# Zero fillings behind the first scaling, and another lane order in a triangular solve: one core, hybrid decoder step

## The chip, the cores and the metric

The kernel runs on one core of a Trainium2 chip. The metric is the device time of one execution in microseconds (us); the time given for a kernel is the median of several executions. The engines are TensorE (PE, with its weight loads listed apart as PEld), VectorE (DVE), ScalarE (ACT), GpSimd (POOL) and SyncE (SP), which issues most transfers.

## The reference

One layer of a decoder over a prompt of 2048 tokens and 8 sequences of 4 new tokens, width 1024, all in fp32. A normalised input `h` is projected to twelve column blocks; a short gated convolution and an RWKV-7 recurrence (16 heads of 64 x 64 state) run beside each other, are gated, projected and added to the input, and a last normalisation follows. What matters here is the recurrence:

```python
def step(S, inp):
    r_t, k_t, v_t, d_t, kk_t, a_t = inp
    sa = jnp.einsum('bhvk,bhk->bhv', S, -kk_t)
    S = (S * d_t[:, :, None, :] + sa[..., None] * (kk_t * a_t)[:, :, None, :]
         + v_t[..., None] * k_t[:, :, None, :])
    y = jnp.einsum('bhvk,bhk->bhv', S, r_t)
    return S, y
```

and the normalisation with which every row begins: `x * rsqrt(mean(x * x) + 1e-6) * g`.

## The kernel before

**Tiling.** The prompt is worked in four sets of 512 tokens. For each set and each pair of heads (8 pairs, so 32 pairs in all) PE projects the columns that the pair needs. Each fp32 product is made of three passes (high part by high part, low by high, high by low), so the operands are split: `XH` and `XL` are the high and low parts of the normalised, transposed input, and `whl` holds both parts of a weight block. A projection is a run of 24 matmuls into a PSUM tile `ip`.

**The recurrence** goes in chunks of 64 tokens, 8 chunks per set. Per pair five stages run as side work between the projections of other columns: `rwkv_keys`, `rwkv_solve`, `rwkv_merge`, `rwkv_load` and `rwkv_chain`. The keys stage makes decayed keys (`AR`, `BK`). The solve stage multiplies them on PE, masks the result into `GM` (on DVE), and inverts the unit triangular matrix of each chunk. It does this in 32 x 32 blocks: a pair has 2 heads x 2 diagonal blocks x 8 chunks = 32 blocks. ACT collects them in `Mc` (the partition holds head, block and row; the free axis chunk and column). DVE transposes `Mc` into `Mi` (128 x 1024, each element copied four times, for four groups of columns), and solves with 31 row steps on DVE: `tt<-Mi,X` multiplies, `X<-X,tt` adds. `X` starts as a copy of the constant `X0`, the identity in the layout of the solve, and holds eight groups of four solved rows. A lane (a partition within a group of 32) stands for one chunk and one of four row offsets. At the end DVE transposes `X` back:

```python
Xo = rw.tile([P, 32, 32], F32, name="Mi")[:, 0:8]
V.transpose(Xo.rearrange("p c (a e) -> p a e c", e=4), X)
```

`Xo` lies in a buffer of the name Mi, so the profile shows this transpose as `Mi<-X`, and the one before the solve as `Mi<-Mc`. Before the change the lane is (row offset e, chunk c), with the chunk running fastest; the transpose back puts chunk c's rows together by writing each element to an address of its own.

`rwkv_merge` copies the four groups of blocks of `Xo` into the block diagonal of `Xbd` on ACT (`Xbd<-Mi`, four copies of 32 x 256), transposes the first ones on DVE (`Mc<-Xbd`), and joins the 32 x 32 inverses to 64 x 64 ones with 32 small matmuls on PE (`pt<-Mc,GM`, then `pt<-Xbd,X`). `rwkv_chain` then carries the state `S` over the chunks: PE makes `pa`, DVE `UB`, PE `pb`, ACT `SV`, PE `pb`, DVE `S`.

**The start.** Four row tiles of 128 tokens are loaded into borrowed buffers (`GM` two, `BKt`, `SV`). ACT sums their squares, DVE and POOL take the root (`nw`, `rstd`), DVE scales one tile and ACT the other (`GM<-GM,rstd`), PE transposes them (`ip<-ident,GM`), and DVE, ACT and POOL split the result into XH and XL. `setup["scaled"][0]` is the DVE scaling of the first tile. `zero_rest` fills with zeros, on POOL, the parts of tiles that later steps read but never write (`UP`, `BK`, `AR`, `Xbd`, `UB`, `SV`, `S`): 18 fillings.

**What sets the order.** Each engine executes its own queue in order. The code records what it issues while a planner (`Clock`) interleaves main work and side work, and DVE and ACT instructions are then fixed in the planned order. `behind_of(b, a)` adds one more rule: instruction b is placed behind a. With `NoSync` this orders queues only; with `Sync` b also waits until a is done. All compute instructions are issued through one helper and so carry the line L264 in the profile; transfers carry L337.

Of the kernel before, what the change touches and what calls it, by code (L numbers as in the profile page):

```python
# [7 lines left out]
F32 = mybir.dt.float32  # L8
# [3 lines left out]
ALU = mybir.AluOpType  # L12
# [4 lines left out]
P = 128  # L17
# [4 lines left out]
NCH = 8  # L22
# [322 lines left out]
def hybrid_kernel(tc, x_prompt, x_sample, state_conv, state_shift, state_rwkv, norm_g, w_in, conv_w,  # L345
# [5 lines left out]
    V, A, G, T = (Traced(e, n, clock) for e, n in ((nc.vector, "DVE"), (nc.scalar, "ACT"), (nc.gpsimd, "POOL"), (nc.tensor, "PE")))  # L351
# [15 lines left out]
    TW = NT + 64  # L367
# [37 lines left out]

    order = []
    raws, parts_, lows = {}, {}, []
    setup = {"casts": [], "lows": [], "scaled": {}}
    state = {"use": 0, "dma": 0, "split": 0}

    def w_advance(dma, split, load):
# [198 lines left out]
    tmp = Ring(ph1.enter_context(tc.tile_pool(name="tmp", bufs=1)), [P, NT + 64], 8, clock)  # L610
# [62 lines left out]
    for hr in range(2):  # L673
        for q in range(2):
            sl = mask_p[hr * 64:(hr + 1) * 64, q]
            G.affine_select(out=sl, in_=sl, pattern=[[1, 64]], compare_op=ALU.is_gt if q == 0 else ALU.is_ge,
                            fill=0.0, base=0, channel_multiplier=-1)
# [3 lines left out]
    for hr in range(2):  # L681
        sl = seqm[hr * 64:(hr + 1) * 64, :]
# [9 lines left out]
                        in1=seqm.unsqueeze(2).broadcast_to([P, NS, SL]), op=ALU.mult)  # L692

    X0 = con.tile([P, 8, 32], F32, name="X0")
    xo0 = tmp.tile([P, TW], F32, name="tmp")[:, 0:256].rearrange("p (a b c) -> p a b c", b=4, c=8)
    G.memset(xo0, 1.0)
    for g in range(4):
        sl = xo0[g * 32:(g + 1) * 32]
        G.affine_select(out=sl, in_=sl, pattern=[[-4, 8], [-1, 4], [0, 8]], compare_op=ALU.is_equal, fill=0.0,
                        base=0, channel_multiplier=1)  # L700
    V.transpose(X0.rearrange("p a b -> p (a b)"), xo0.rearrange("p a b c -> p (a b c)"))
    tmp.free(xo0)

    rst = con.tile([P, NT], BF16, name="rst")
# [496 lines left out]
    col = [slice(32 * b, 32 * b + 32) for _ in range(2) for b in range(2)]  # L1201
    blk = [(slice(64 * h + 32 * b, 64 * h + 32 * b + 32)) for h in range(2) for b in range(2)]

    def rwkv_solve(th, p, o):

        AR = o["AR"]
        samp = th == LAST
        GM = GMB[(th * NB + p) % 2]


        yield 0.0, (), 2
        for c0 in range(0, NCH + samp, 4):
            cs = range(c0, min(NCH + samp, c0 + 4))
            pp = [new_pt([P, 512], F32, name="pt") for _ in range(2)]
            for c in cs:
                for h in range(2):
                    T.matmul(pp[h][:, (c - c0) * P:(c - c0 + 1) * P], lhsT=BK[HS[h], c].rearrange("p q t -> p (q t)"),
                             rhs=AR[HS[h], c].rearrange("p q t -> p (q t)"), start=True, stop=True)
            k = len(cs)
            mk = mask_s if c0 == NCH else mask_p  # L1220
            for h in range(2):
                V.tensor_tensor(out=GM[:, c0:c0 + k, :, h, :],
                                in0=pp[h][:, 0:k * P].rearrange("p (c a t) -> p c a t", a=2, t=64),
                                in1=mk.unsqueeze(1).broadcast_to([P, k, 2, 64]), op=ALU.mult)
            yield W["score"], (), 2 if c0 + 4 < NCH + samp else 0


        Mc = rw.tile([P, NCH, 32], F32, name="Mc")
        for i, g in enumerate(blk):
            h, b = i // 2, slice(i % 2 * 32, i % 2 * 32 + 32)  # L1230
            A.copy(Mc[g], GM[b, 0:NCH, 0, h, b])
        yield 0.5, [Mc]
        Mi = rw.tile([P, 32, 32], F32, name="Mi")
        V.transpose(Mi.rearrange("p t (e c) -> p t e c", c=NCH),
                    Mc.rearrange("p c t -> p t c").unsqueeze(2).broadcast_to([P, 32, 4, NCH]))
        X = rw.tile([P, 8, 32], F32, name="X")
        A.copy(X, X0)
        Mo = rw.tile([P, NCH, 32], F32, name="Mo")
        A.copy(Mo[64:96], GM[0:32, 0:NCH, 0, 1, 32:64])
        yield W["inv0"], [Mi, X]  # L1240

        for j in range(31, 0, -1):
            c0 = j // 4
            if c0 == 7:
                V.scalar_tensor_tensor(out=X[:, 7, 0:j], in0=Mi[:, j, 0:j], scalar=X[:, 7, j:j + 1], in1=X[:, 7, 0:j],
                                       op0=ALU.mult, op1=ALU.add)
                yield W["inv"]
                continue
            tt = sm.tile([P, 80], F32, name="tt")
            tv = tt[:, 0:(8 - c0) * j].rearrange("p (c i) -> p c i", i=j)  # L1250
            V.tensor_tensor(out=tv, in0=Mi[:, j, 0:j].unsqueeze(1).broadcast_to([P, 8 - c0, j]),
                            in1=X[:, c0:8, j:j + 1].broadcast_to([P, 8 - c0, j]), op=ALU.mult)
            V.tensor_tensor(out=X[:, c0:8, 0:j], in0=X[:, c0:8, 0:j], in1=tv, op=ALU.add)
            yield W["inv"]
        Xo = rw.tile([P, 32, 32], F32, name="Mi")[:, 0:8]
        V.transpose(Xo.rearrange("p c (a e) -> p a e c", e=4), X)
        o.update(GM=GM, Xo=Xo, Mo=Mo)
        yield W["inv"]

    def rwkv_merge(th, p, o):  # L1260

        GM, Xo, Mo = (o[k] for k in ("GM", "Xo", "Mo"))
        Xbd = o["Xbd"] = XB[(th * NB + p) % 2]
        samp = th == LAST
        for i, g in enumerate(blk):
            A.copy(Xbd[g, 0:NCH, col[i]], Xo[g])

        T11 = rw.tile([P, NCH, 32], F32, name="Mc")
        V.transpose(T11[0:96], Xbd[0:96, 0:NCH, col[0]])
        yield W["bt"], [T11[0:96], Mo[64:96]], 1  # L1270
        Wm = rw.tile([P, 8, 32], F32, name="X")
        pt = new_pt([P, 512], F32, name="pt")
        for c in range(NCH):
            for h in range(2):
                T.matmul(pt[blk[2 * h + 1], c * 32:(c + 1) * 32], lhsT=Mo[64:96, c, :] if h else GM[0:32, c, 0, 0, 32:64],
                         rhs=T11[blk[2 * h], c, :], start=True, stop=True)
        for h in range(2):
            A.copy(Wm[blk[2 * h + 1]], pt[blk[2 * h + 1], 0:NCH * 32].rearrange("p (c t) -> p c t", t=32))
        yield W["bt"], [Wm[32:128], Xbd[32:128]], 1
        pt = new_pt([P, 512], F32, name="pt")  # L1280
        for c in range(NCH):
            for h in range(2):
                T.matmul(pt[blk[2 * h], c * 32:(c + 1) * 32], lhsT=Wm[blk[2 * h + 1], c, :],
                         rhs=Xbd[blk[2 * h + 1], c, col[1]], start=True, stop=True)
        for h in range(2):
            A.copy(Xbd[blk[2 * h], 0:NCH, col[1]],
                   pt[blk[2 * h], 0:NCH * 32].rearrange("p (c t) -> p c t", t=32))
        yield W["bt"], (), samp
        if samp:
            for h in range(2):  # L1290
                V.tensor_copy(Xbd[HS[h], NCH, HS[h]], GM[0:64, NCH, 0, h, :])

            M = Xbd[:, NCH, :]
            pt = new_pt([P, 512], F32, name="pt")
            T.transpose(pt[:, 0:P], M, ident)
            MT = sm.tile([P, P], F32, name="sq")
            A.copy(MT, pt[:, 0:P])
            V.tensor_tensor(out=M, in0=M, in1=ident, op=ALU.add)
            yield W["samp"], [M, MT], 1
            for _ in range(SL - 2):  # L1300
                pt = new_pt([P, 512], F32, name="pt")
                T.matmul(pt[:, 0:P], lhsT=MT, rhs=M, start=True, stop=True)
                V.tensor_tensor(out=M, in0=pt[:, 0:P], in1=ident, op=ALU.add)
                yield W["samp"], [M], 1
        yield W["merge"], [Xbd]
# [440 lines left out]
    St = [xp.tile([P, P], F32, name=f"S{p}") for p in range(NB)]  # L1746
# [6 lines left out]
    scv = xp.tile([P, NB, 2 * NS], F32, name="scv")  # L1753
    def zero_rest():
        for t in (UP[64:128, 1].bitcast(F32), UP[0:64, 3].bitcast(F32), BK[:, NCH], ARB[0][:, NCH], ARB[1][:, NCH], *XB, *UB, SV[:, NCH]):
            G.memset(t, 0.0)
        for p in range(NB):
            G.memset(St[p], 0.0)
        yield 1

    def end_(th, p):
# [35 lines left out]
    for th, hv, p, nx in plan:  # L1797
# [15 lines left out]
        e = EDGE / 2 * NB  # L1813
# [15 lines left out]
    SP.flush(0)  # L1829
    clock.planning = False  # L1830

    def behind_of(b, a):
        tc.add_manual_dep(b, a.name, mybir.DependencyInfo(
            mybir.DependencyClass.NoSync, mybir.DependencyReason.DATA), reason="keep_in_program_order")

    for ops in clock.begun.values():
        ops.sort(key=lambda o: o[0])
        for (_, a), (_, b) in zip(ops, ops[1:]):
            behind_of(b, a)
    for b in setup["lows"]:  # L1840
        behind_of(b, setup["scaled"][0])
    behind_of(setup["casts"][1], setup["scaled"][1])

    ph1.close()
# [372 lines left out]
```

## Time and profile before

| | |
|---|---|
| median of 3 runs | 3048.32 us (3045.91 to 3054.13) |
| the profiled execution's own time | 3047.81 us |
| its span, first to last instruction | 3046.1 us |
| mean granted TensorE clock | 0.997 |
| POOL, DVE, ACT busy | 316.0, 2162.4, 1346.3 us |

A row of a group reads: engine, operation, output<-inputs by the program's names, shape, count, then busy us, mean ns of one, and the idle time of the engine before them with what ended it. A row of the timeline reads: start in us, length in us, engine, instruction, and in brackets the idle time before it. A row of stretches reads: from:to, length, then busy us and count for PE, PEld, DVE, ACT and POOL, the granted PE clock, the DMA share and GB/s.

### The profile page before, as it was taken

To read this page: it belongs to the slowest core of one execution; us is meant where nothing else is said; L and a number is where in the kernel's file an instruction comes from. 1 tells how busy PE (TensorE), PEld (TensorE's weight loads), DVE (VectorE), ACT (ScalarE), POOL (GpSimd) and SP (SyncE) were. 2 spreads that over 40 slices of the span, in tenths; PEclk is the share of its full clock that TensorE was granted. 3 is DMA by queue.
4 is the path that set the end of the run, shared out by engine and by line. 5 is a ranking of instruction groups with operands and counts; after the bars stand their busy time and mean duration, and the time that the engine had idled before them with its cause. 6 is when DMAs were issued, how large, how long until landed. Compare 5 with 4: busy or idle time off the path is not lost. (4 is left out here: it accounts for less than half of the span.)

```text
span 3046.1 us, 56137 instructions
## 1 busy us (share of the span) xinstructions
PE 2986.0 (98%) x21370; PEld 2559.5 (84%) x21370; DVE 2162.4 (71%) x5504; ACT 1346.3 (44%) x2745; POOL 316.0 (10%) x520
## 2 busy tenths in 40 slices
PE   8999999999999999999999999999999999999998
PEld 6778777788888788788787899999999997888996
DVE  6777778767777777777777777667767744486575
ACT  4555555554444445444444444444444322324223
POOL 2011111011111111111111110000100000000000
PEclk9999999999999999999999999999999999999999
DMA  8877767766666667666666665444343588898775
GB/s 273 289 236 237 251 220 248 230 223 228 208 218 210 209 218 240 223 222 216 216 221 212 198 215 179 149 136 146 127 145 130 170 267 317 325 324 295 271 264 195
DMA packets 319731, 678.05 MB, mean 223 GB/s; under 512 B 47610, under 2 KB 179827, under 8 KB 269798
## 3 DMA queue, kind: packets, MB, share of 16 engines
q1 hardware_dynamic: 310758, 670.27, 64.9%
q10 hardware_dynamic: 8704, 4.20, 0.5%
q8 instruction: 169, 2.77, 0.4%
q14 instruction: 100, 0.82, 0.1%
HBM read 479.10 MB, written 195.28 MB: 221 GB/s over the span
## 5 line engine op out<-in xcount | busy, mean ns | idle before, releaser
L264 PE MATMUL ip<-XH,whl 128*128 128x512 f32 (+3 forms) x6832 | 1853.9, 351 | 5.8 <-DVE whl L264 3.8
L264 PEld LDWEIGHTS ip<-XH,whl 128*128 128x128 f32 x6832 | 1174.5, 189 | 137.1 <-DVE whl L264 6.8
L264 PE MATMUL ip<-XL,whl 128*128 128x512 f32 (+3 forms) x3416 | 1195.4, 350 | 0.0
L264 PEld LDWEIGHTS ip<-XL,whl 128*128 128x128 f32 x3416 | 646.8, 189 | 65.0 <-issue 5.5
L264 DVE SCALAR_TENSOR_TENSOR S<-pb,pe,sp 64x64 f32<-64x64 f32 x512 | 143.1, 279 | 98.1 <-PE pb L264 91.5
L264 DVE TENSOR_TENSOR X<-X,tt 128x60 f32<-128x60 f32 (+21 forms) x864 | 187.7, 217 | 27.9
L264 DVE TENSOR_TENSOR tt<-Mi,X 128x60 f32<-128x60 f32 (+21 forms) x864 | 188.9, 219 | 24.9
L264 ACT ACTIVATE sp<-S,pe 128x128 f32<-128x128 f32 x256 | 102.4, 400 | 205.6 <-DVE S L264 204.5
L264 ACT COPY SV<-pb 64x128 f32<-64x128 f32 x256 | 66.1, 258 | 283.8 <-PE pb L264 279.7
L264 DVE TENSOR_TENSOR UB<-pa,P 64x64 f32<-64x64 f32 x512 | 110.2, 215 | 109.9 <-PE pa L264 92.3
L264 ACT ACTIVATE tmp<-ip,vec 128x512 f32<-128x512 f32 (+2 forms) x174 | 103.0, 593 | 181.0 <-PE ip L264 175.7
L264 PE MATMUL acc<-XH,whl 128*128 128x264 f32 (+1 forms) x800 | 141.2, 329 | 0.5 <-DVE tmp L264 0.5
L264 PEld LDWEIGHTS acc<-XH,whl 128*128 128x128 f32 x800 | 119.0, 188 | 14.9 <-DVE tmp L264 0.7
L264 PE MATMUL acc<-UA,whl 128*128 128x264 f32 (+1 forms) x720 | 117.7, 324 | 1.9 <-DVE My L264 1.9
L264 PEld LDWEIGHTS pb<-UB,Xbd 128*128 128x128 f32 x512 | 85.0, 188 | 40.1 <-PE ip L264 15.5
L264 PEld LDWEIGHTS acc<-UA,whl 128*128 128x128 f32 x720 | 105.0, 190 | 13.4 <-DVE My L264 2.3
L264 DVE TENSOR_TENSOR whl<-wraw,whl 128x1024 fp32r<-128x1024 f32 x81 | 101.7, 1255 | 19.6 <-ACT whl L264 18.9
L264 DVE TENSOR_TENSOR GM<-pt,mask_p 128x512 f32<-128x512 f32 x128 | 82.6, 686 | 42.9 <-PE pt L264 42.5
L264 PE MATMUL pb<-UB,Xbd 128*128 128x128 f32 x512 | 105.0, 286 | 8.1 <-DVE UB L264 7.0
L264 PEld LDWEIGHTS pa<-S,AR 128*128 128x128 f32 x512 | 86.7, 188 | 26.3 <-DVE S L264 14.7
L264 PE MATMUL acc<-XL,whl 128*128 128x264 f32 (+1 forms) x616 | 108.6, 326 | 0.0
L264 PEld LDWEIGHTS pb<-SV,BKt 128*128 128x128 f32 x512 | 89.4, 188 | 20.6 <-ACT SV L264 6.5
(559 smaller groups left out, 4422.9 us busy)
## 6 DMA issues: line engine op xcount, KB each, us to landing
wraw<-in_w_in_dram SPq DMA_DIRECT2D x81, 512.0 KB
whl<-w_k SPq DMA_DIRECT2D x24, 1024.0 KB
whl<-w_r SPq DMA_DIRECT2D x24, 1024.0 KB
whl<-w_v SPq DMA_DIRECT2D x24, 1024.0 KB
whl<-w_z SPq DMA_DIRECT2D x24, 1024.0 KB
whl<-w_xin SPq DMA_DIRECT2D x24, 1024.0 KB
whl<-w_cg SPq DMA_DIRECT2D x24, 1024.0 KB
whl<-w_zc SPq DMA_DIRECT2D x24, 1024.0 KB
```

What stands on the lines that cost most here:

```text
L264: r = f(*a, **k)
```

## The change

Two things. The zero fillings of `zero_rest` wait (with a semaphore) until the first row tile has been scaled on DVE. And the lane of the solve becomes (chunk c, row offset e), with e fastest, so a chunk's four solved rows stand in neighbouring lanes. The constant `X0` is made to fit. The transpose into `Mi` now reads each element of `Mc` four times in succession, the transpose back is plain, and the ACT copies into `Xbd` bring the rows into order by reading runs of four elements.

```diff
-    xo0 = tmp.tile([P, TW], F32, name="tmp")[:, 0:256].rearrange("p (a b c) -> p a b c", b=4, c=8)
+    xo0 = tmp.tile([P, TW], F32, name="tmp")[:, 0:256].rearrange("p (a c b) -> p a c b", b=4, c=8)
...
-        G.affine_select(out=sl, in_=sl, pattern=[[-4, 8], [-1, 4], [0, 8]], compare_op=ALU.is_equal, fill=0.0,
+        G.affine_select(out=sl, in_=sl, pattern=[[-4, 8], [0, 8], [-1, 4]], compare_op=ALU.is_equal, fill=0.0,
...
         Mi = rw.tile([P, 32, 32], F32, name="Mi")
-        V.transpose(Mi.rearrange("p t (e c) -> p t e c", c=NCH),
-                    Mc.rearrange("p c t -> p t c").unsqueeze(2).broadcast_to([P, 32, 4, NCH]))
+        V.transpose(Mi.rearrange("p t (c e) -> p t c e", c=NCH),
+                    Mc.rearrange("p c t -> p t c").unsqueeze(3).broadcast_to([P, 32, NCH, 4]))
...
         Xo = rw.tile([P, 32, 32], F32, name="Mi")[:, 0:8]
-        V.transpose(Xo.rearrange("p c (a e) -> p a e c", e=4), X)
+        V.transpose(Xo.rearrange("p a b -> p (a b)"), X.rearrange("p a b -> p (a b)"))
...
         for i, g in enumerate(blk):
-            A.copy(Xbd[g, 0:NCH, col[i]], Xo[g])
+            A.copy(Xbd[g, 0:NCH, col[i]].rearrange("p c (a e) -> p c a e", e=4),
+                   Xo[g].rearrange("p a (c e) -> p c a e", e=4))
...
     def zero_rest():
         for t in (UP[64:128, 1].bitcast(F32), ..., *XB, *UB, SV[:, NCH]):
-            G.memset(t, 0.0)
+            r = G.memset(t, 0.0)
+            setup["zeros"].append(r.ins)
         for p in range(NB):
-            G.memset(St[p], 0.0)
+            setup["zeros"].append(G.memset(St[p], 0.0).ins)
...
+    for b in setup["zeros"]:
+        behind_of(b, setup["scaled"][0], mybir.DependencyClass.Sync)
     for b in setup["lows"]:
         behind_of(b, setup["scaled"][0])
```

No instruction changes its place in any queue. On POOL, at the start, the first filling has one more semaphore to wait for, that of DVE; the other fillings and the XL subtractions stand behind it in the same queue. The piece of the difference (`UP` is the first filled tile, `rstd` the root, `carry` a one-column copy):

```order
@@ -26,5 +26,5 @@
 L264 TENSOR_TENSOR rstd<-nw_285,mhalf 128x2 [waits DVE_49,Pool_49]
 L264 COPY tmp<-carry 128x1
-L264 MEMSET UP 64x128 [waits Pool_49]
+L264 MEMSET UP 64x128 [waits DVE_49,Pool_49]
 L264 MEMSET UP 64x128
 L264 MEMSET BK 128x128 [waits Pool_49]
```

Nothing moved; the second filling and all behind it now start after the DVE scaling.

On DVE, at the end of the first pair's solve, the last row step (`tt`, `X`), the transpose back (`Mi<-X`) and the merge's transpose (`Mc<-Xbd`) stand as before; only the shape of the write differs:

```order
@@ -166,5 +166,5 @@
 L264 TENSOR_TENSOR tt<-Mi,X 128x8 [waits DVE_49]
 L264 TENSOR_TENSOR X<-X,tt 128x8 [waits DVE_49]
-L264 STREAM_TRANSPOSE Mi<-X 128x32x8 [waits DVE_49]
+L264 STREAM_TRANSPOSE Mi<-X 128x256 [waits DVE_49]
 L264 SCALAR_TENSOR_TENSOR tmp<-ip,omu,tmp 128x512 [waits Activation_49,Pool_49]
 L264 STREAM_TRANSPOSE Mc<-Xbd_218 96x256 [waits Activation_49]
```

Nothing moved here either, and it is the same in the other 31 pairs.

More of the change, by code (lines that the diff above doesn't have):

```diff
@@ L407, in hybrid_kernel @@
     raws, parts_, lows = {}, {}, []
-    setup = {"casts": [], "lows": [], "scaled": {}}
+    setup = {"casts": [], "lows": [], "scaled": {}, "zeros": []}
     state = {"use": 0, "dma": 0, "split": 0}
@@ L698, in hybrid_kernel @@
         sl = xo0[g * 32:(g + 1) * 32]
-        G.affine_select(out=sl, in_=sl, pattern=[[-4, 8], [-1, 4], [0, 8]], compare_op=ALU.is_equal, fill=0.0,
+        G.affine_select(out=sl, in_=sl, pattern=[[-4, 8], [0, 8], [-1, 4]], compare_op=ALU.is_equal, fill=0.0,
                         base=0, channel_multiplier=1)
-    V.transpose(X0.rearrange("p a b -> p (a b)"), xo0.rearrange("p a b c -> p (a b c)"))
+    V.transpose(X0.rearrange("p a b -> p (a b)"), xo0.rearrange("p a c b -> p (a c b)"))
     tmp.free(xo0)
@@ L1830, in hybrid_kernel, with behind_of @@
     clock.planning = False
-    def behind_of(b, a):
-        tc.add_manual_dep(b, a.name, mybir.DependencyInfo(
-            mybir.DependencyClass.NoSync, mybir.DependencyReason.DATA), reason="keep_in_program_order")
+    def behind_of(b, a, kind=mybir.DependencyClass.NoSync):
+        tc.add_manual_dep(b, a.name, mybir.DependencyInfo(kind, mybir.DependencyReason.DATA), reason="keep_in_program_order")
     for ops in clock.begun.values():
```

## The prediction

> **What bounds the kernel now.** I read the page first (busy shares, then the chain that ended last), then who waited for whom on TensorE, then two places in the timeline: the start, and the end of one pair's triangular solve.
>
> ```profile
> span 3046.1 us, 56137 instructions
> PE 2986.0 (98%) x21370; PEld 2559.5 (84%) x21370; DVE 2162.4 (71%) x5504; ACT 1346.3 (44%) x2745; POOL 316.0 (10%) x520
> ```
>
> TensorE (PE) is busy for 2986.0 of 3046.1 us, and the change takes no matmul away. So it can gain only from the 60.1 us in which PE stands idle, and from stretches in which PE's clock is low. Who ends the idle time of PE:
>
> ```profile
> PE ip L264 <- DVE GM L264: 11.2, 1, 11.2
> PE pt L264 <- DVE Mc L264: 7.3, 9, 2.1
> PE pb L264 <- DVE UB L264: 7.0, 17, 1.3
> PE ip L264 <- DVE whl L264: 3.8, 5, 1.3
> PE pa L264 <- DVE S L264: 3.3, 8, 0.8
> PE pt L264 <- DVE Yc L264: 2.5, 4, 1.2
> ```
>
> (us in total, times, longest.) The first row is the start: PE waits for the scaled rows in GM. The second is the merge: its first small matmuls wait for Mc, the transposed blocks that the solve leaves. These two rows lie straight behind the two edited places. The other four are waits for VectorE (DVE) in general.
>
> **The start.** DVE has to finish the root of the rows' mean square (nw, rstd) and scale the rows (GM) before PE can transpose them. DVE first, then GpSimd (POOL) with the zero fillings, then PE:
>
> ```profile
> 9.03 3.14 DVE L264 TENSOR_SCALAR nw<-nw 128x2 f32<-128x2 f32 x1
> 12.20 0.16 DVE L264 TENSOR_TENSOR rstd<-rstd,nw 128x2 f32<-128x2 f32 x1
> 12.40 1.33 DVE L264 TENSOR_SCALAR GM<-GM,rstd 128x1024 f32<-128x1024 f32 x1
> ...
> 22.55 0.17 DVE L264 TENSOR_SCALAR nw<-nw 128x2 f32<-128x2 f32 x1
> ...
> 22.96 0.75 DVE L264 TENSOR_SCALAR BKt<-BKt,rstd 128x1024 f32<-128x1024 f32 x1
> ```
>
> ```profile
> 8.81 0.45 POOL L264 MEMSET UP<- 64x128 f32 x2
> ...
> 12.08 1.79 POOL L264 MEMSET S<- 128x128 f32 x8
> 18.09 1.27 POOL L264 TENSOR_TENSOR XL<-tmp,XH 128x512 fp32r<-128x512 f32 x1 [4.22 <-ACT XH L264]
> ```
>
> ```profile
> 13.79 3.67 PE L264 MATMUL ip<-ident,GM 128*128 128x128 f32 x16 [11.15 <-DVE GM L264]
> ...
> 19.42 0.58 PE L264 MATMUL ip<-XL,whl 128*128 128x256 f32 x1
> ```
>
> A two-element operation on DVE takes 3.14 us while POOL fills zeros; the same one, 13 us later, takes 0.17 us. Scaling 128x1024 takes 1.33 us beside the fillings and 0.75 us without. The fillings cost DVE 2.97 + 0.58 = 3.55 us. With the change they wait for that scaling, so DVE is done at 13.73 - 3.55 = 10.18 us and PE's first transposes start near 10.25 instead of 13.79.
>
> Part of it is given back. POOL's fillings take 8.81 to 13.87 = 5.06 us; from 10.25 they end at 15.3. Behind them in POOL's queue stands the XL subtraction (18.09). Its input would be ready at 18.09 - 3.55 = 14.55, so it starts 0.8 us late, and the matmul that reads XL (19.42), the third of the first block, is released only then. The first user of a zeroed tile is the transfer into UP at 60.6 us, 45 us after the fillings' new end (first and last start behind the median time):
>
> ```profile
> L337 SPq DMA_DIRECT2D UP<-up x128: 319/486/1390, 60.6 to 2275.0; - x128
> ```
>
> The change issues no transfer and moves none, so the DMA queue of SyncE keeps its row. Net: 3.55 - 0.8 = 2.7 us. The loads don't stand in the way: the transfer engines had run dry before 12 us:
>
> ```profile
> 12.00:13.00 1.00, 0.00 (x0) 0.00 (x0) 0.93 (x3) 0.54 (x1) 1.00 (x8) 1.00 0.00 1
> ```
>
> Bounds: 3.55 if the subtraction's lateness is covered, 1.0 if the fillings, now beside busy DVE work, run half as long again (5.06 x 1.5 ends 2.5 us later). I take 2.7, since the fillings ran beside DVE work in the old place too.
>
> **The layout of the solve.** It touches 32 pairs of heads; per pair two DVE transposes and four ScalarE (ACT) copies change their access patterns. Their rows, with mean ns behind the bar, and beside them rows of the same engine with other patterns:
>
> ```profile
> L264 DVE STREAM_TRANSPOSE Mi<-Mc 128x1024 f32<-128x1024 f32 x32 | 66.0, 2063 | 13.9 <-ACT Mc L264 13.6
> L264 DVE STREAM_TRANSPOSE Mi<-X 128x256 f32<-128x256 f32 x32 | 20.8, 650 | 0.9
> L264 DVE STREAM_TRANSPOSE Mc<-Xbd 96x256 f32<-96x256 f32 x32 | 14.1, 440 | 13.7 <-ACT Xbd L264 13.5
> ...
> L264 ACT COPY Xbd<-Mi 32x256 f32<-32x256 f32 x128 | 51.7, 404 | 40.5 <-DVE Mi L264 38.9
> L264 ACT ACTIVATE cv<-u,cwh 128x512 f32<-128x512 f32 x32 | 23.1, 723 | 37.5 <-DVE u L264 37.4
> L264 ACT ACTIVATE cv<-u,cwh 128x32 f32<-128x32 f32 x8 | 2.5, 317 | 0.0
> ```
>
> Mi<-X (the solved rows turned back) writes single elements 128 bytes apart today and takes 650 ns; Mc<-Xbd has 256 elements in a row too, in runs of 32, and takes 440. After the change Mi<-X is plain, so 440: 0.21 us less.
>
> Mi<-Mc reads elements 128 bytes apart. At 2063 ns for 1024 elements it takes 1.9 ns each above some 0.17 us of fixed time (440 less 256 at 1.05); that is the rate of the scattered Mi<-X, (650 - 170) / 256 = 1.9. After the change each element is read four times running before the next one. Bounds: 0 gained if only a true run of addresses counts, 2063 - (170 + 1024 x 1.05) = 0.82 us if four hits are enough. I take 0.82, since the row that it resembles in speed is slow by its stride alone. Per pair DVE has 1.03 us less.
>
> The ACT copies write runs of 32 as before but read runs of four. The sample's tap (cv<-u, 128x32) reads runs of four as well; against 128x512 in long runs it takes (723 - 317) / 480 = 0.85 ns per element for the difference, which leaves 290 ns fixed and nothing for the short runs. So I take 404 ns as before; the other end is DVE's ratio, 1.9/1.05 on the part above ACT's fixed time (404 less 256 at 0.85 is 186): 186 + 218 x 1.8 = 580 ns.
>
> [...]
>
> **What of it reaches PE.** The end of a solve in the pair that waits longest, and the state of the engines and the clock around two such places:
>
> ```profile
> 644.40 0.63 DVE L264 STREAM_TRANSPOSE Mi<-X 128x256 f32<-128x256 f32 x1
> ...
> 645.06 1.66 ACT L264 COPY Xbd<-Mi 32x256 f32<-32x256 f32 x4 [1.60 <-DVE Mi L264]
> 646.32 0.44 DVE L264 STREAM_TRANSPOSE Mc<-Xbd 96x256 f32<-96x256 f32 x1 [0.78 <-ACT Xbd L264]
> ...
> 646.91 0.18 PE L264 MATMUL pt<-Mc,GM 32*32 32x32 f32 x1 [2.06 <-DVE Mc L264]
> ```
>
> ```profile
> 508.42 0.18 PE L264 MATMUL pt<-Mc,GM 32*32 32x32 f32 x1 [1.71 <-DVE Mc L264]
> ```
>
> ```profile
> 2389.10:2410.00 20.90, 20.90 (x196) 20.70 (x195) 18.87 (x72) 5.00 (x12) 0.00 (x0) 1.00 0.71 226
> 615.30:644.40 29.10, 27.09 (x245) 25.82 (x245) 27.26 (x86) 14.29 (x26) 5.97 (x8) 1.00 0.87 285
> 646.90:651.30 4.40, 4.39 (x50) 4.28 (x51) 2.54 (x6) 3.02 (x6) 0.30 (x2) 0.61 0.20 28
> ```
>
> Last transpose, three of the four copies, transpose back, PE: a straight chain, so its 0.21 us counts in full wherever PE waits for Mc. The 0.82 us lie 20 to 30 us earlier; they reach the end as far as DVE is full in between, and in the two stretches above (columns: length, PE, its loads, DVE) it is, for 18.87 of 20.90 and 27.26 of 29.10 us. Each of the nine waits can lose up to 1.03 us: 2.06 and 1.71 keep 1.03 and 0.68, the other seven can go: 7.3 - 1.71 = 5.6 us. I take 4.5, because behind the wait others in the same pair are uncovered, and DVE isn't quite full. The waits for UB, S, Yc and whl (16.6 us) come from a DVE queue that is behind; it gets 33 of 2162 us shorter, and only some of them stand soon after a Mi transpose: a tenth, 1.5 us. Together 6.0 us. Bounds: 9 x 0.21 = 1.9 down to 1 if only the last transpose helps and part is taken again; 11 if all 32 pairs' waits between their two transposes could use their 1.03 us.
>
> After the 2.06 us gap the granted clock reads 0.61 of full speed for 4.4 us, so 1.7 us of PE's work is lost. With a gap of 1 us this may not happen: half of it, 0.8 us.
>
> **Sum.** 2.7 + 6.0 + 0.8 = 9.5 us. The profiled execution took 3047.8 us (span 3046.1 and 1.7 around it), so 3038.3; the median of the runs, 3048.3, lies 0.5 above. I predict 3039 us.
>
> **Rivals.**
> 1. *The big transpose isn't slow by its stride* but by its size; it stays at 2063 ns. For it: no contiguous transpose of 1024 elements is in the trace. Against it: the scattered one of 256 has the same 1.9 ns. Then the waits give 1.5 us, sum 4: 3044 us. Chance 0.10.
> 2. *ACT's copies pay for runs of four*: 580 ns, three on the chain, 0.53 us of each 1.03 gone. Half of 6.0 stays: 2.7 + 3 = 5.7, 3042 us. The tap's row speaks against it. Chance 0.09.
> 3. *The start's gain comes to little*, because PE's slow phase lasts longer. These rows show it:
>
> ```profile
> 18.70:22.70 4.00, 3.99 (x17) 3.76 (x18) 2.98 (x8) 3.10 (x5) 2.91 (x5) 1.00 0.98 277
> 28.00:34.00 6.00, 6.00 (x53) 6.00 (x52) 5.86 (x19) 2.71 (x5) 1.51 (x2) 1.00 0.36 98
> ```
>
>    The same 256-column matmuls take 0.235 us each (3.99 / 17) before 22.7 us and 0.113 us later; the slow phase costs half of its length. If it ends at the same moment although PE starts 2.7 us earlier, 1.35 of the 2.7 us are lost, and with 1.7 of the 6 lost in other waits the time is 3042 us. Chance 0.06. [...]
> 4. *More than I count*: in stretches where DVE is full throughout, a wait that goes uncovers none, and 11 us come out of the waits, with 3.5 at the start and 1.7 of clock: 3032 us. Chance 0.09.
> 5. *Slower.* The copies' short reads cost more than the transposes save. Place: between Mi<-X and Mc<-Xbd, in all 32 pairs. Three copies stand against 1.03 us, so it turns at 404 + 340 = 744 ns a copy; to end 0.3% (9 us) above, the 2.7 us of the start included, some 12 waiting pairs have to lose 1 us each, which needs copies of 1080 ns, 3.5 ns per element, where the slowest row of this kind has 1.9. Time 3058 us. Chance 0.06.
>
> **How the numbers follow.** 0.3% (9.1 us, so below 3039.2 or above 3057.5) is about what a measurement of this kernel can tell from no change. My forecast has 0.60 and its own range, 3033 to 3044, straddles that line: 0.33 below, 0.27 above. With rival 4 faster has 0.42; with rivals 1, 2 and 3 the same has 0.52; slower is rival 5, 0.06. The range goes from 3033 (a third of rival 4 left in) to 3047 (start 1.0 and waits 1.0 alone give 3046): it leaves out rival 5, most of rival 4 and the odd run.
>
> **What would show it.** Start: the two-element operation at 9.03 us near 0.17 us, PE's first transposes before 10.5 us, fillings up to 15.3 us, the first XL matmul near 16.7 us. If that is still near 19, the fillings have found another victim. Layout: Mi<-Mc near 1.24 us, Mi<-X near 0.44 us, Xbd<-Mi at 0.40 us. PE's row for Mc should fall from 7.3 to near 3 us. If the transposes shrink and this row doesn't, the 0.82 us are lost in DVE's idle time; if the row shrinks but others grow by as much, the waits have only changed hands.

## The result, and the profile after

The changed kernel takes 3028.98 us (median; 3028.52 to 3033.76), against 3048.27 us for the kernel before on the same chip (3044.76 to 3054.13). The ratio is 0.9939, with a 95% interval from 0.9926 to 0.9952. That is 19.3 us less, twice the 9.5 us forecast, and 4 us below the range. The profiled execution took 3028.97 us, so its rows can be set against the 3047.81 us of the execution shown before: 18.8 us between the two.

First the page of the changed kernel, its span and its busy times:

```profile
span 3027.3 us, 56138 instructions
PE 2975.2 (98%) x21370; PEld 2558.6 (85%) x21370; DVE 2132.4 (70%) x5504; ACT 1344.6 (44%) x2745; POOL 314.4 (10%) x520
```

PE stands idle for 3027.3 - 2975.2 = 52.1 us, where it was 60.1: 8.0 us less. But the span is 18.8 us shorter. The other 10.8 us came out of PE's *busy* time, 2986.0 to 2975.2, with the same 21370 matmuls. This is the line on which the prediction fell, and most of the rest is about it.

Who ended PE's idle time in the changed kernel (us in total, times, longest):

```profile
PE ip L264 <- DVE GM L264: 8.1, 1, 8.1
PE pb L264 <- DVE UB L264: 6.8, 15, 1.1
PE pt L264 <- DVE Mc L264: 4.5, 7, 1.5
...
PE ip L264 <- DVE whl L264: 2.7, 4, 1.3
...
PE pa L264 <- DVE S L264: 2.4, 7, 0.5
PE ip L264 <- POOL XL L264: 2.3, 3, 1.2
...
PE pt L264 <- DVE Yc L264: 1.6, 4, 0.9
```

The start's row fell from 11.2 to 8.1, Mc's from 7.3 to 4.5, the four general ones from 16.6 to 13.5, and a new one, POOL's XL, appeared with 2.3.

The start in the timeline of the changed kernel:

```profile
9.69 0.17 DVE L264 TENSOR_SCALAR nw<-nw 128x2 f32<-128x2 f32 x1
...
10.09 0.75 DVE L264 TENSOR_SCALAR GM<-GM,rstd 128x1024 f32<-128x1024 f32 x1
...
10.90 3.36 PE L264 MATMUL ip<-ident,GM 128*128 128x128 f32 x16 [8.11 <-DVE GM L264]
10.97 0.45 POOL L264 MEMSET UP<- 64x128 f32 x2 [1.56 <-DVE GM L264]
...
14.24 1.24 POOL L264 MEMSET S<- 128x128 f32 x8
15.44 1.28 POOL L264 TENSOR_TENSOR XL<-tmp,XH 128x512 fp32r<-128x512 f32 x1
...
16.77 0.39 PE L264 MATMUL ip<-XL,whl 128*128 128x256 f32 x1 [0.48 <-POOL XL L264]
```

The two-element operation takes 0.17 us where it took 3.14, the scaling 0.75 where it took 1.33. PE's first transposes start at 10.90 and not at 13.79. The fillings now start at 10.97 and end at 15.48, and POOL's subtraction, which stands behind them in the queue, starts at 15.44 (times on POOL are rough). So the matmul that reads XL comes at 16.77 where it came at 19.42: 2.65 us.

The groups of the solve in the changed kernel (busy us, mean ns of one, idle time before them):

```profile
L264 ACT COPY Xbd<-Mi 32x256 f32<-32x256 f32 x128 | 51.6, 403 | 32.4 <-DVE Mi L264 30.8
...
L264 DVE STREAM_TRANSPOSE Mi<-Mc 128x1024 f32<-128x1024 f32 x32 | 39.8, 1243 | 13.5 <-ACT Mc L264 13.2
L264 DVE STREAM_TRANSPOSE Mi<-X 128x256 f32<-128x256 f32 x32 | 14.2, 444 | 0.9
```

2063 became 1243 ns, 650 became 444, and the copies stayed at 403. Every duration came out as forecast, so the miss lies in what of them reaches the end.

### Where the other 10.8 us were

Here is one place in the middle of a solve. PE runs projection matmuls (`ip<-XH,whl`) and then needs UB, which DVE makes for the chain of the pair before. DVE's queue holds Mi<-Mc, then S and nine row steps, then UB. The kernel before:

```profile
702.59 2.05 DVE L264 STREAM_TRANSPOSE Mi<-Mc 128x1024 f32<-128x1024 f32 x1 [0.53 <-ACT Mc L264]
...
708.80 0.45 DVE L264 TENSOR_TENSOR UB<-pa,P 64x64 f32<-64x64 f32 x2
...
708.99 0.40 PE L264 MATMUL ip<-XH,whl 128*128 128x512 f32 x1
709.36 0.30 PEld L264 LDWEIGHTS pb<-UB,Xbd 128*128 128x128 f32 x2 [0.41 <-issue]
709.39 0.46 PE L264 MATMUL pb<-UB,Xbd 128*128 128x128 f32 x2
```

and the same instructions in the changed kernel:

```profile
694.73 1.25 DVE L264 STREAM_TRANSPOSE Mi<-Mc 128x1024 f32<-128x1024 f32 x1 [0.52 <-ACT Mc L264]
...
700.26 0.45 DVE L264 TENSOR_TENSOR UB<-pa,P 64x64 f32<-64x64 f32 x2
...
701.14 0.39 PE L264 MATMUL ip<-XH,whl 128*128 128x512 f32 x1
701.14 0.42 PEld L264 LDWEIGHTS pb<-UB,Xbd 128*128 128x128 f32 x2
701.37 0.38 PE L264 MATMUL pb<-UB,Xbd 128*128 128x128 f32 x2
```

Before, `pb<-UB` started 0.40 us behind the projection matmul in front of it; after, 0.23 us. UB is written until 709.25 us, and only then can its weight load begin (709.36, with 0.41 us of idle time before it on the load side); after the change UB is done at 700.71 and the load runs ahead. So PE had a wait of 0.17 us for UB, yet the row of `pb<-UB` has no bracket with idle time. Matmuls of 512 columns start every 0.23 us here, but the profile gives each a length of 0.40, so the listed lengths overlap by 0.17 us. A wait of up to some 0.17 us behind such a matmul therefore counts as busy. So PE's "busy 98%" holds small waits for DVE too, and the column of idle time knows nothing of them. A wait shows as time between *starts*.

The spacing between the starts of neighbouring matmuls, taken over all 21370 of them in both traces and summed by the instruction that came late, has these largest gains (us; the second column is what the idle time in brackets shows of it):

```
                 spacing   listed idle
pb<-UB,Xbd         4.4        0.7
pt<-Mc,GM          3.4        3.0
ip<-ident,GM       3.2        3.0     (the start)
acc<-UA,whl        2.7        1.1
ip<-XH,whl         2.6        1.1
pa<-S,AR           1.9        0.9
ip<-ident,wraw     1.6        1.0
ip<-XL,whl        -2.2       -2.3     (the new waits for POOL)
```

Of the 4.4 us at `pb<-UB` the brackets show 0.7: the other 3.7 were hidden. The surplus at `acc<-UA` is something else, the clock.

PE's granted clock falls to one half for stretches of 3.41 us, and each costs half its length (in the one at 2555.8 us the `acc<-UA` matmuls start 0.43 us apart, behind it 0.23). Past the start the kernel before has three of them, at 647.7, 2026.7 and 2555.8 us, and the changed one has one, at 2010.6 us: 3.4 us less are lost. First two of the kernel before; then, of the changed kernel, the one that it has, and the place at 639.8 us that had one before and now runs at full clock (length, then busy us and count of PE, PEld, DVE, ACT, POOL, granted clock, DMA share, GB/s):

```profile
2026.70:2030.10 3.40, 3.40 (x20) 3.17 (x20) 1.04 (x3) 0.17 (x1) 0.00 (x0) 0.50 0.46 81
...
2555.80:2559.20 3.40, 3.40 (x9) 2.63 (x9) 3.40 (x4) 0.49 (x1) 0.00 (x0) 0.50 1.05 401
```

```profile
2010.60:2014.00 3.40, 3.40 (x16) 3.40 (x17) 1.04 (x3) 1.29 (x4) 0.00 (x0) 0.50 0.26 82
...
639.80:643.20 3.40, 3.36 (x54) 3.23 (x55) 1.76 (x5) 2.12 (x4) 0.18 (x1) 1.00 0.41 128
```

The changed kernel also shows half clock from 17.2 to 20.6 us. That is no loss against the kernel before, which ran the same matmuls of the start just as slowly: between 18.7 and 22.7 us its clock column reads 1.00, but a matmul of 256 columns took 0.235 us there and 0.113 later, as the rows under rival 3 of the prediction show. So the start has to be set apart. Here both executions are cut at the same matmul, 60.11 us into the kernel before and 57.36 us into the changed one:

```profile
0.00:60.11 60.11, 45.16 (x266) 40.36 (x267) 37.43 (x78) 30.63 (x46) 20.04 (x61) 1.00 0.79 262
60.11:3046.09 2985.98, 2940.81 (x21105) 2519.17 (x21103) 2125.01 (x5426) 1315.67 (x2699) 295.93 (x459) 1.00 0.66 222
```

```profile
0.00:57.36 57.36, 44.41 (x267) 39.84 (x268) 34.92 (x79) 30.52 (x46) 20.75 (x61) 0.97 0.80 276
57.36:3027.25 2969.89, 2930.82 (x21105) 2518.74 (x21103) 2097.48 (x5426) 1314.08 (x2699) 293.62 (x459) 1.00 0.66 223
```

The start gives 2.8 us. The stretch behind it is 16.1 us shorter (2985.98 to 2969.89), and 10.0 of these are busy time of PE (2940.81 to 2930.82). The 18.8 us then divide so: the start 2.8, listed idle time behind it 6.1, clock 3.4, and waits hidden in busy time 10.0 - 3.4 = 6.6.

### The profile page after: what moved, and what is told of

Same layout as the page of the kernel before. It is cut to its first block, busy times and chain, and to the rows that moved or that the text cites. A ratio compares the mean times of both kernels' runs of the same rounds, so it can differ in the third digit from the quotient of the medians.

```text
span 3027.3 us, 56138 instructions
## 1 busy us (share of the span) xinstructions
PE 2975.2 (98%) x21370; PEld 2558.6 (85%) x21370; DVE 2132.4 (70%) x5504; ACT 1344.6 (44%) x2745; POOL 314.4 (10%) x520
## 5 line engine op out<-in xcount | busy, mean ns | idle before, releaser
L264 DVE TENSOR_TENSOR whl<-wraw,whl 128x1024 fp32r<-128x1024 f32 x81 | 101.7, 1256 | 19.5 <-ACT whl L264 18.8
L264 PEld LDWEIGHTS pb<-SV,BKt 128*128 128x128 f32 x512 | 89.3, 188 | 20.6 <-ACT SV L264 6.6
```

Of the source, the lines that this page charges most:

```text
L264: r = f(*a, **k)
```

## The experiments

Theory: DVE's shorter transposes also remove waits that the idle column doesn't list, so about 0.4 of every microsecond taken from the solve reaches the end. Rival: only listed idle time can be won, and the surplus comes from somewhere else (the start, the clock, another execution). All ratios are against the kernel before, run with each on the same chip.

### The kernel before, once more

No edit: one more execution, for the scatter between executions.

> The kernel before, profiled once more, for the spread between two executions of one program. Theory A (the waits that the layout removes are larger than the idle time shows): span within 4 us of 3046.1, the start and the solve unchanged, PE's row for Mc again near 7.3 us. Theory B (part of the gain is the luck of the transfers at the start of the last phase): PE's wait for the first sums of that phase (acc<-UA, 1.86 us before, 0.73 us after) differs here from 1.86 by more than 0.5 us, and so does the span by 1 to 3 us.

3051.31 us, span 3049.6, 3.5 us above the execution shown first. The waits are much the same (Mc 7.4 us in 9, UB 7.1 in 17). The difference is the clock: half-speed stretches of 17.1 us in all where the first execution has 10.2. With half their length taken off, the spans are 3041.1 and 3041.0. So the clock makes the difference between these two; one pair doesn't show how well spans with the half-speed stretches taken out compare elsewhere. On this measure the changed kernel has 3023.9, or 3025.6 if its stretch at 17.2 us stays in, since the slow start of the kernel before isn't taken out either: a gain of 17.1 or 15.4.

### Each half alone

The fillings wait, with the old layout (the layout's lines of the change put back; two of the places):

```diff
-        V.transpose(Xo.rearrange("p a b -> p (a b)"), X.rearrange("p a b -> p (a b)"))
+        V.transpose(Xo.rearrange("p c (a e) -> p a e c", e=4), X)
...
-                   Xo[g].rearrange("p a (c e) -> p c a e", e=4))
+            A.copy(Xbd[g, 0:NCH, col[i]], Xo[g])
```

> The zero fillings wait for the scaling, the solve keeps its old layout. Theory A: only the start moves, by the 2.65 us that the matmul reading XL moved (19.42 to 16.77), so 0.1% below the kernel before, 3045.6 against 3048.3; Mi<-Mc stays at 2063 ns, PE's row for Mc near 7.3 us. Rival (the earlier start grows on its way, since weights and transfers run ahead): 6 us or more below the kernel before.

3043.38 us, ratio 0.9988 (0.9979 to 0.9997): 3.7 us by the ratio, 5.1 by the medians, 3.9 by the span without its half-speed stretches (3037.1). Busy time and waits of this kernel:

```profile
PE 2984.6 (98%) x21370; PEld 2557.3 (84%) x21370; DVE 2160.8 (71%) x5504; ACT 1345.0 (44%) x2745; POOL 314.0 (10%) x520
```

```profile
PE ip L264 <- DVE GM L264: 7.5, 1, 7.5
```

The start's wait falls as in the full change, and PE's busy time by 1.4 us only. The new layout, with the fillings in the old place:

```diff
-    for b in setup["zeros"]:
-        behind_of(b, setup["scaled"][0], mybir.DependencyClass.Sync)
```

> The new lane order alone, the zero fillings at their old place. Theory A: 3032 us, 16 us below the kernel before; the start as before (PE's first transposes at 13.8 us); Mi<-Mc 1243 ns, Mi<-X 444 ns. Rival (the start's gain grows): at most 12 us below.

3033.64 us, ratio 0.9956 (0.9943 to 0.9968): 13.4 us by the ratio.

```profile
PE 2978.9 (98%) x21370; PEld 2561.1 (84%) x21370; DVE 2136.6 (70%) x5504; ACT 1344.2 (44%) x2745; POOL 314.4 (10%) x520
```

```profile
PE ip L264 <- DVE GM L264: 11.8, 1, 11.8
...
PE pt L264 <- DVE Mc L264: 5.4, 7, 1.9
```

Mc's wait gives 1.9 us and the busy time 7.1. These 7.1 us aren't clock: the half-speed stretches of this execution come to 10.2 us, as in the kernel before, and the slow matmuls of its start end at 23 us in both. So the hidden waits stand here without the clock. The halves add up within their intervals, some 4 us to each side (3.7 + 13.4 = 17.1 against 18.6 by ratio), so the surplus is mainly the layout's: 1.03 us shorter in each of 32 solves, 33 us of DVE, and 13.4 of them arrive, a factor of 0.41 (0.30 to 0.53 by the interval).

### Where the runs of four are paid

DVE writes runs of four words and ACT copies plainly, the other way round from the change:

```diff
-        V.transpose(Xo.rearrange("p a b -> p (a b)"), X.rearrange("p a b -> p (a b)"))
+        V.transpose(Xo.rearrange("p c (a e) -> p a c e", e=4), X)
...
-            A.copy(Xbd[g, 0:NCH, col[i]].rearrange("p c (a e) -> p c a e", e=4),
-                   Xo[g].rearrange("p a (c e) -> p c a e", e=4))
+            A.copy(Xbd[g, 0:NCH, col[i]], Xo[g])
```

> The changed kernel, but the transpose back writes runs of four to the final order and ACT copies runs of 32 as before the change. If runs of 16 bytes cost DVE nothing when written: Mi<-X stays near 444 ns, ACT's copy at 403 ns, time the same as the changed kernel (within 1 us). If only long runs are written at full rate: Mi<-X near 650 ns and some 2 us slower than the changed kernel.

3027.73 us, ratio 0.9937 (0.9925 to 0.995), the transpose 445 ns, the copies 404. Runs of four words cost nothing on either engine (445 ns written so by DVE, 444 plain; 403 read so by ACT, 404 in long runs), and the two versions can't be told apart.

The copies walk the rows in an order that takes a new place for each word, on both sides; within each eight words the reads step by 128 bytes and the writes by 16:

```diff
-            A.copy(Xbd[g, 0:NCH, col[i]].rearrange("p c (a e) -> p c a e", e=4),
-                   Xo[g].rearrange("p a (c e) -> p c a e", e=4))
+            A.copy(Xbd[g, 0:NCH, col[i]].rearrange("p c (a e) -> p c e a", e=4),
+                   Xo[g].rearrange("p a (c e) -> p c e a", e=4))
```

(The planner's cost for these copies was held, so that the order of work is that of the changed kernel.) The question is whether ACT pays for a new place with each word.

> [...] If ACT pays for that as DVE's transposes do: a copy takes 580 to 620 ns instead of 403, the chain from Mi<-X to Mc grows by some 0.6 us per pair, and the time by 3 to 7 us over the changed kernel. If ACT doesn't pay: 403 ns and the changed kernel's time within 1 us. The order of DVE, ACT, PE and POOL is that of the changed kernel.

3053.78 us, ratio 1.0019 (1.001 to 1.0028), 24.8 us above the changed kernel and slower than before. The copies' group, and PE's wait:

```profile
L264 ACT COPY Xbd<-Mi 32x256 f32<-32x256 f32 x128 | 85.0, 664 | 32.6 <-DVE Mi L264 31.0
```

```profile
PE pt L264 <- DVE Mc L264: 17.4, 22, 2.2
```

A copy takes 261 ns more; three of them on the chain in 32 solves are 25.1 us, and 24.8 arrive by the medians, 18.7 to 20.4 by the spans without half-speed stretches (3044.3 here). The expected 3 to 7 us were far too low. This stretch, last transpose to copies to Mc, passes on three quarters or more: PE waits there in 22 solves and not in 7. So the turning point of rival 5, put at 744 ns a copy, lies below 664.

### The two transposes, one at a time

On top of the scattered copies, first the old layout of `Mi<-Mc` alone (slow_in), then a scattered write of `Mi<-X`, 32 bytes from word to word (slow_back); the constant and the copies' reads follow:

```diff
+        V.transpose(Mi.rearrange("p t (e c) -> p t e c", c=NCH),
+                    Mc.rearrange("p c t -> p t c").unsqueeze(2).broadcast_to([P, 32, 4, NCH]))
```

```diff
+        V.transpose(Xo.rearrange("p a b -> p (a b)").rearrange("p (b a) -> p a b", a=8), X)
```

> Old lane order, so Mi<-Mc reads scattered words (2063 ns), but the transpose back is plain (444 ns), and ACT's copies read words 32 bytes apart to put the rows in order. To be held against act_scattered, which differs in Mi<-Mc alone. Theory A (the 0.82 us of the transpose in are worth most of the gain, since PE's waits behind a full DVE queue are hidden in its busy time): 8 to 10 us slower than act_scattered. Rival (the forecast's view: only the listed waits for Mc count): 4 us slower or less.

> New lane order and fast transpose in (1243 ns), but the transpose back writes words 32 bytes apart; ACT's copies read words 32 bytes apart. To be held against act_scattered, which differs in Mi<-X alone. [...] If the distance matters, Mi<-X lies between 444 and 650 ns.

slow_in: 3067.48 us, ratio 1.0065 (1.0052 to 1.0077). `Mi<-Mc` is back at 2064 ns, `Mi<-X` stays at 445, the copies take 684. The span without half-speed stretches is 3053.6, 9.3 above the scattered copies alone (3044.3), for 26 us of added DVE time and some 2 us in the copies: about a third. By the medians it is 13.7 us, a half. slow_back: 3064.16 us, ratio 1.005 (1.0036 to 1.0064). Its transpose and PE's wait:

```profile
L264 DVE STREAM_TRANSPOSE Mi<-X 128x256 f32<-128x256 f32 x32 | 22.0, 687 | 0.9
```

```profile
PE pt L264 <- DVE Mc L264: 22.0, 24, 2.5
```

and its span without half-speed stretches 3050.5, 6.2 above, for 0.242 us in 32 solves = 7.7: eight tenths. By the medians it is 10.4 us, more than was added: this execution has 23.9 us at half speed, that of the scattered copies 13.7. So the size of the factor hangs on the measure, but on either one a microsecond at the end of the chain is worth over twice one at its head.

### A longer transpose in the changed kernel

The same two places, without the scattered copies' load: the changed kernel with one transpose issued twice.

```diff
         V.transpose(Xo.rearrange("p a b -> p (a b)"), X.rearrange("p a b -> p (a b)"))
+        nc.vector.transpose(Xo.rearrange("p a b -> p (a b)"), X.rearrange("p a b -> p (a b)"))
```

> The changed kernel with the transpose Mi<-X issued twice in each of the 32 solves, the second time plain and on the same buffers: 0.44 us more on VectorE in each solve, 14.2 us in all, at the end of the chain of a solve, where the ScalarE copies and the transpose Mc<-Xbd wait for it. The orders of the engines stay but for a handful of rows. Theory (waits that the idle column does not list count too): 0.4 of it to all of it reaches TensorE, so 6 to 14 us over the changed kernel, a ratio to the kernel before of 0.9957 to 0.9985, with TensorE's busy sum up by 2 us or more at the same 21370 matmuls, and the wait for Mc up from 4.5 to 8 us or more. Rival (the listed waits alone count): the listed wait for Mc grows by 0.44 us at the 7 places that wait already, 3.1 us, and TensorE's busy sum stays within 1 us of 2975.2.

3037.97 us, ratio 0.9969 (0.9957 to 0.998), 9.0 us above the changed kernel for 14.2 us added.

```profile
PE 2977.8 (98%) x21370; PEld 2560.0 (84%) x21370; DVE 2147.8 (71%) x5536; ACT 1345.6 (44%) x2745; POOL 315.0 (10%) x520
```

```profile
PE pt L264 <- DVE Mc L264: 9.2, 17, 1.5
```

Busy time rises by 2.6 us, idle time by 6.4, and both executions have one half-speed stretch behind the start. At the end of the chain most of the loss is listed. The other one:

```diff
+        nc.vector.transpose(Mi.rearrange("p t (c e) -> p t c e", c=NCH),
+                    Mc.rearrange("p c t -> p t c").unsqueeze(3).broadcast_to([P, 32, NCH, 4]))
```

> The changed kernel with the transpose Mi<-Mc issued twice in each of the 32 solves: 1.24 us more on VectorE in each, 39.8 us in all, at the start of a solve, 40 to 60 us ahead of the rows that need its result. Some 25 rows of VectorE and 90 of TensorE stand elsewhere. Theory (a late queue of VectorE holds TensorE up by amounts that the idle column does not list, about 0.4 of the added time as with the transpose taken from 2.06 to 1.24 us): 12 to 20 us over the changed kernel, a ratio to the kernel before of 0.9975 to 1.0005, TensorE's busy sum up by 5 us or more. Rival (the start of a solve is far ahead of what needs it, only the listed waits for Mc count): 0.44 of 4.5 us and no more, 4 us or less over the changed kernel, busy sum unchanged.

3048.19 us, ratio 0.9997 (0.9989 to 1.0006): 19.2 us above the changed kernel by the medians, for 39.8 us added, 0.48.

```profile
PE 2990.3 (98%) x21370; PEld 2557.5 (84%) x21370; DVE 2167.9 (71%) x5536; ACT 1345.4 (44%) x2745; POOL 315.6 (10%) x520
```

```profile
PE pb L264 <- DVE UB L264: 6.9, 25, 0.6
PE pt L264 <- DVE Mc L264: 6.1, 9, 1.5
```

The span is 19.3 us longer, the idle time 4.2, the busy time 15.1, with the same matmuls. Behind the start this execution has two half-speed stretches where the changed kernel has one. Cut at the same matmul as above, the busy time behind the start is 14.4 us longer, 12.7 without that stretch, against 5.0 of listed idle time. The spacing of starts grew most ahead of `pa<-S` (6.4 us, 1.8 of them listed) and `pb<-UB` (6.1 us, 0.4 listed). This is the surplus of the change, run backwards; the rival allowed 4 us or less in all. One reserve: in both of these kernels about a twentieth of DVE's rows (258 and 279 of 5504) stand elsewhere in its queue, more than was expected, so the added instruction isn't the only difference. The place shown above, in this kernel:

```profile
703.21 0.40 PE L264 MATMUL ip<-XH,whl 128*128 128x512 f32 x1
703.83 0.46 PE L264 MATMUL pb<-UB,Xbd 128*128 128x128 f32 x2 [0.22 <-DVE UB L264]
```

From start to start 0.62 us, against 0.23 in the changed kernel: `pb<-UB` came 0.39 us later, and the bracket tells 0.22 of it.

### Two ways to go on

The fillings behind four of POOL's XL subtractions, on the version in which DVE writes the fours, so that POOL's new wait at the start goes:

```diff
-        behind_of(b, setup["scaled"][0], mybir.DependencyClass.Sync)
+        behind_of(b, setup["lowparts"][3])
```

> The kernel dve_writes_fours with the zero fillings behind POOL's four XL subtractions of the first set instead of ahead of them. Theory A: the XL subtraction no longer waits for the fillings (0.5 to 0.9 us at the first matmul that reads XL), the rest as in dve_writes_fours: 3027 us, not to be told from it. Rival: the fillings now collide with the second half of the rows and PE waits there: 1 us or more above it.

3033.2 us, ratio 0.9948 (0.9936 to 0.9961), against 0.9937 for the version that it was put on: not better. The first XL matmul came at 16.51 us, but by 30 us nothing was left of that, and by 50 us it is 1.7 us behind that version. The fillings, now at 28.2 to 32.8 us, met another small operation of DVE, which takes 0.35 us in that version, and PE waited for DVE behind it:

```profile
28.30 3.30 DVE L264 COPY lws<-lwh 64x8 f32<-64x8 f32 x2
```

```profile
PE ip L264 <- DVE kT L264: 1.4, 1, 1.4
```

This is what the rival expected. Another 4.5 us come in between 2500 and 2600 us, where PE waits for My and a half-speed stretch stands:

```profile
PE acc L264 <- DVE My L264: 3.2, 1, 3.2
```

The four copies in the order of blocks 0, 2, 1, 3, on the same version:

```diff
-        for i, g in enumerate(blk):
+        for i, g in sorted(enumerate(blk), key=lambda x: x[0] % 2):
```

> The version that writes Mi<-X in runs of four and copies Xbd<-Mi plainly, with the four ScalarE copies of a solve in the order of blocks 0, 2, 1, 3 and not 0, 1, 2, 3. The rows that the following matmuls take from the transpose Mc<-Xbd come from blocks 0 and 2, so it has to wait for two copies or three and the second pair of matmuls for the rest. The planner shifts the order of work on every engine because of it, so the run tells what this version is worth and not the copies alone. Theory (the chain transpose, copies, Mc goes about one to one into the time where it is late): if a copy of 0.40 us leaves the chain, 3 to 8 us less than the changed kernel, a ratio to the kernel before of 0.991 to 0.993. Rival (what is left in the waits is VectorE's queue, and not the copies): within 1.5 us of the version with its copies in the old order, 0.9937.

3038.12 us, ratio 0.9966 (0.9953 to 0.9979), 10 us worse. The transpose Mc<-Xbd does wait less for ACT, 7.7 us where it was 13.0 in the changed kernel, and PE less for Mc (3.4 us), but more for UB:

```profile
L264 DVE STREAM_TRANSPOSE Mc<-Xbd 96x256 f32<-96x256 f32 x32 | 14.1, 440 | 8.3 <-ACT Xbd L264 7.7
```

```profile
PE pb L264 <- DVE UB L264: 9.3, 16, 2.8
```

But the planner had moved about a fifth of DVE's rows, so what the copies alone are worth stays open. Nothing that ran beats the changed kernel by more than the measurement can tell.

## Why the prediction was wrong

**Start, 2.7 us: right, with some luck.** The two-element operation, the scaling and the first XL matmul (16.77 for 16.7) came as worked out; 2.65 us at that matmul, 2.8 at 60 us. Two slips cancelled in it. PE's first transposes were to start at 10.25 and started at 10.90, since DVE's chain to `nw` ran some 0.65 us later, and the fillings started as much later; but they took 4.5 us and not the 5.06 of their old place, and so ended at 15.48 for 15.3. The lower bound of 1.0 for this term doesn't follow from its own numbers: with 0.8 + 2.5 us given back of 3.55, 0.2 is left. Rival 3 (the slow phase eats the gain) did not come: the slow matmuls ended earlier too, at 20.6 instead of 23.1 us, and the lead is still there at 60 us.

**Durations of the layout: right**, to 4 ns. Rival 1 (slow by size) fell with 1243 ns, rival 2 (ACT pays for runs of four) with 403 ns. The 1.05 ns per element that the estimate used stands in the kernel before (`Y<-Y,Y` of 128x1024 takes 1219 ns, `Rx<-Rx,fg` of 128x512 takes 682: 537 / 512) and comes back in the two transposes of the change: (1243 - 444) / (1024 - 256) = 1.04. That four reads of one word in succession would be as fast as a plain run was a choice between two bounds, since the kernel before has no such transpose; 1243 ns decided it. The other access patterns that ran: four words written in a row 445 ns, a word every 32 bytes 687, every 128 bytes 650 (DVE, 256 elements); a copy on ACT 403 ns when it reads runs of four, 664 when its reads step by 128 bytes and its writes by 16. They show that scattered words are slow and runs of four are not; what in the memory makes it so they don't show.

**"It can gain only from the 60.1 us in which PE stands idle, and from stretches in which PE's clock is low": this step failed.** Some 6.6 us came from busy time at full clock that was waiting in disguise, 7.1 in the kernel with the layout alone, and a transpose issued twice put 12.7 back in. The quantities that the step left out stood in the trace: `pb<-UB` starting 0.40 us behind a matmul whose like are 0.23 us apart.

**What of the layout reaches PE, 6.0 us: mis-sized.** Listed idle time behind the start gave 6.1 us, as much as the 6.0; but the term stood for the whole effect, and that was 6.1 + 6.6 = 12.7. That the 6.1 fits is partly luck: the 4.5 for Mc was 2.8, the 1.5 for UB, S, Yc and whl was 3.1, My gave 1.2, POOL's XL took 1.8 back, and small rows make up the rest. Of the two longest waits, 2.06 us was to keep 1.03 and kept 1.13, but 1.71 was to keep 0.68 and kept 1.49:

```profile
502.57 0.18 PE L264 MATMUL pt<-Mc,GM 32*32 32x32 f32 x1 [1.49 <-DVE Mc L264]
...
639.84 0.18 PE L264 MATMUL pt<-Mc,GM 32*32 32x32 f32 x1 [1.13 <-DVE Mc L264]
```

This does not mean that the solve gained little. PE itself arrives earlier, at 501.08 us where it came at 506.71, as the start and waits ahead of it have become shorter, and then waits again: a listed wait shows the race between the two, and not what the solve gained.

**Clock, 0.8 us: mis-sized,** 3.4 in the profiled executions. The stretch behind the wait at 646.9 us went, as this term half hoped, and so did the one at 2555.8, which the prediction put at nothing: PE's wait for My ahead of it fell from 1.86 to 0.7 us, and 2.7 us of lead were won there. Between executions the clock scatters by more than that (5.1 and 8.5 us lost in two of the kernel before), so this term can't be settled by one pair.

**Rival 4 (more than I count)** came near in time, 3032 against 3029, but not by its mechanism: it let 11 us come out of the listed waits, and they gave 6.1. It was capped by the same step as the main sum. **Rival 5 (slower)** did not come, since the copies stayed at 403 ns; it was right in its place and wrong in its price. It set 0.34 us more in each copy against 1.03 us less in the transposes, as if both arrived alike. By the medians the runs show 1.0 for the copies and 0.41 for the transposes: the changed kernel's 19.3 us are used up by 19.3 / 32 / 3 = 0.20 us a copy, at some 605 ns, and 664 ns ended 5.5 us above the kernel before. Its 12 waiting solves were 22.

## What to carry to other kernels

A bound of "idle time of the busiest engine" is no bound where that engine's listed lengths overlap (here 0.40 us long, 0.23 us from start to start): compare the spacing of starts with the spacing of like instructions that wait for nothing, and count the difference as waiting. Where an engine's queue is full and feeds the busy one in many small steps, price what is taken out of the queue by a factor measured by adding (issue one instruction twice and see what arrives), here 0.3 to 0.5 at the head of the chain, 0.6 or more at the last transpose, and 0.75 to 1.0 for the copies behind it. Before two executions are compared, see whether the clock column shows the slow clock of the start in both. A shorter listed wait is the outcome of a race between two engines that both got faster, so a single one says little about the gain.

## What was not expected of the hardware

- ACT pays for scattered words as DVE does: (664 - 186) / 256 = 1.87 ns per word, with the 186 ns of fixed time worked out in the prediction, where DVE has 1.9. With only the reads scattered (slow_in) a copy took 684 ns.
- Zero fillings on POOL slowed a DVE operation of a few elements twice: 3.14 us for 0.17 at the start of the kernel before, 3.30 for 0.35 (two copies) where the fillings came last.
- A shorter distance didn't help: words 32 bytes apart took 687 ns in `Mi<-X`, words 128 bytes apart 650.
- PE's clock fell to half for stretches of 3.41 us. Of the three of the kernel before, the second execution has two at the same places of the work and lacks the third; in its stead it has one of some 10 us (granted clock 0.96 from 500 to 510 us and 0.52 from 510 to 520), at a place where the first waits 1.71 us for Mc and runs on at full clock. The ones at 2026.7 and 2010.6 us stand behind no idle time over 0.3 us, those at 647.7 and 2555.8 behind 2.06 and 1.86 us. So the idle time ahead doesn't decide it in these traces: two of these four stretches had less than 0.3 us of it and none more than 2.06, and behind the wait of 1.71 us the first execution has no stretch. What sets them off isn't shown.
